# Where the split activations lie in on-chip memory: from in front of the small tiles to behind them

## The chip, the cores and the metric

The kernel runs on one core of a Trainium2 chip. The time is that of one execution on the device, in microseconds, as the median of several runs. Before the change it is 1981.72 us, the median of 3 runs from 1981.64 to 1981.88 us.

## What is computed

A decoder layer on 256 tokens of width 2048, in float32. A feed-forward layer, a mixer of two kinds of heads, and a second feed-forward layer stand one after the other, each behind a norm and added to the residual stream; a last norm follows.

```python
y = swiglu(rmsnorm(x, g1), w_gate1, w_up1, w_down1);  x = x + 0.5 * y      # 2048 -> 5632 -> 2048
y = hybrid_mixer(rmsnorm(x, g2), w_in, ..., w_out);   x = x + y            # 2048 -> 8192 columns, 2048 -> 2048
y = swiglu(rmsnorm(x, g3), w_gate2, w_up2, w_down2);  x = x + 0.5 * y
out = rmsnorm(x, final_norm)

def swiglu(h, w_gate, w_up, w_down):
    return (jax.nn.silu(h @ w_gate) * (h @ w_up)) @ w_down
```

The mixer is a retention with 4 heads and a gated linear recurrence with 8 heads on one joint projection of 8192 columns. Nearly all the work is in the products with the weights.

## The kernel before

Activations are kept transposed, a k-tile being 128 features on the partitions by 256 tokens. To multiply in nearly full float32 precision, each operand is split into a high and a low part of type fp32r, and three of the four products of parts are summed: high by high, high by low, low by high. The weights come in blocks of 128 x 1024 float32 (512 KB), one transfer each, from the SP queue into one of 6 buffers `raw` (L134). ScalarE (ACT) rounds a block to `whi` (L152), VectorE (DVE) subtracts to get `wlo` (L153); there are 4 buffers of each. Loads run 6 blocks ahead of the splits and splits up to 4 blocks ahead of the products, in the order of one flat list of (unit, block).

The split activations stand in three tiles, each with the high part and the low part of a k-tile side by side (2 x 256 columns): `xs` (16 k-tiles, 32768 bytes on each partition), written by `split_to` (L219, L220) and read by the gate and up products of both feed-forward layers and by the mixer's input projection; `hs` (44 k-tiles), read by the down products; `ms` (16 k-tiles), read by the mixer's output projection.

`run_seq` issues the products, unit by unit and block by block. A unit is one group of output columns.

- Kind T gives [columns, tokens]: the weights are stationary and the activations stream. For each k-tile and each half of the columns, L188 multiplies `whi` with both parts (512 columns in one matmul) and L189 multiplies `wlo` with the high part (256 columns). On the last k-tile the two are L191 and L192, in the other order. The last unit of the kernel uses L184 to L186 for one of its halves.
- Kind N gives [tokens, columns], for the mixer's values and output gates: a part of the activations is stationary (128 tokens) and 512 columns of `whi` or `wlo` stream, in L201, L202 and L203.

In the first stages blocks of two units (three at the start) alternate; in the down stage one unit follows the other. The norm's 1/rms is applied to the results, so products need not wait for it. `tick` counts a planned time with every product and lets the evacuation of earlier results, the mixer's small products (L615, L616, L637, L690 and others) and the splits of the next operand be issued between the products when they are due.

Tiles are laid out in the order in which their pools and they themselves are allocated: first the pool `cp` with `xT` (the residual stream), `xs` and the small tiles, then the pool `wp` with `raw`, `whi` and `wlo`, then `ev` for results, then the pool of the stage with `hs`, or `mg`, `ms` and the mixer's tiles. In the built program, in bytes on a partition:

| tile | address | remainder of 256 | with the change |
|---|---|---|---|
| xT | 16512 | 128 | the same |
| xs | 32896 | 128 | 38112, remainder 224 |
| gain, ident, ones, onesr, acc, rn, mh, rb, lb, ol, lm, le1, le0 | 65664 to 70879 | 128 for gain, 0 for ident, ones, onesr, acc | 32896 to 38111, the same remainders |
| raw (6 of 4096) | from 70880 | 224 | the same |
| whi (4 of 4096) | from 95456 | 224 | the same |
| wlo (4 of 4096) | from 111840 | 224 | the same |
| the split of e (L610, L612) | from 128256 | 0 | the same |
| hs | 136512 | 64 | the same |
| ms | 152896 | 64 | the same |

Each k-tile of `xs`, `hs` and `ms` is 2048 bytes, each stationary tile of `whi` or `wlo` 512 bytes, so every tile that one matmul reads starts at its buffer's remainder.

Of the kernel before, what the change touches and what calls it, by code (L numbers as in the profile page):

```python
# [7 lines left out]
F32 = mybir.dt.float32  # L8
F32R = mybir.dt.float32r
# [6 lines left out]
P = 128  # L16
D = 2048
S = 256
FF = 5632
KD = D // P  # L20
# [11 lines left out]


class Unit:
    """One group of output columns: kind T gives [cols, tokens], kind N gives [tokens, cols]."""

    def __init__(self, kind, w, col, ktiles, src, evac):
        self.kind, self.w, self.col, self.kt = kind, w, col, ktiles
# [6 lines left out]
class Layer:  # L45
# [14 lines left out]
            pass  # L60

    def tick(self, ns):
        """Products run without a pause; the work that hangs on them is emitted between them when it is due."""
        self.clock += ns
        due = [t for t in self.tasks if t[0] <= self.clock]
        for t in due:
            self.tasks.remove(t)
            self._step(t)
# [5 lines left out]
    def build(self):  # L74
        nc, tc, ctx, a = self.nc, self.tc, self.ctx, self.a
        cp = ctx.enter_context(tc.tile_pool(name="cp", bufs=1))
        self.wp = ctx.enter_context(tc.tile_pool(name="wp", bufs=1))
        self.ev = ctx.enter_context(tc.tile_pool(name="ev", bufs=4))
        self.pu = ctx.enter_context(tc.tile_pool(name="pu", bufs=3, space=bass.MemoryType.PSUM))
        self.pm = ctx.enter_context(tc.tile_pool(name="pm", bufs=2, space=bass.MemoryType.PSUM))  # L80
        self.xT = cp.tile([P, KD, S], F32, name="xT")
        self.xs = cp.tile([P, KD, 2, S], F32R, name="xs")
        self.gain = cp.tile([P, 6, KD], F32, name="gain")
        self.ident = cp.tile([P, P], F32, name="ident")
        self.ones = cp.tile([P, P], F32, name="ones")
        self.onesr = cp.tile([P, P], F32R, name="onesr")
        self.acc = cp.tile([P, 2, S], F32, name="acc")
        self.rn = cp.tile([P, 2], F32, name="rn")
        self.mh = cp.tile([P, 4], F32, name="mh")
        self.rb = cp.tile([P, S], F32, name="rb")  # L90

        ffn = lambda i: self.ffn_units(i)
        f1 = ffn(1)
        mx = self.mix_units()
        f2 = ffn(2)
        self.sched = f1 + mx + f2
        flat = []
        for kind, item in self.sched:
            if kind == "seq":
                flat += item  # L100
        self.flat = flat
        self.n_dma = 0
        self.n_split = 0
        self.blocks = {}
        self.pos = 0

        nc.gpsimd.memset(self.ones, 1.0)
        nc.vector.memset(self.acc[:, 0, :], 0.0)
        nc.gpsimd.memset(self.mh, -0.5)
        nc.vector.tensor_copy(self.onesr, self.ones)  # L110
        nc.sync.dma_start(self.gain, a["gains"])
        self.ahead_dma(1)
        for c in range(1, 8):
            self.x_load(c)
            self.ahead_dma((0, 2, 3, 4, 5, RAW_BUFS, RAW_BUFS, RAW_BUFS)[c])
        nc.sync.dma_start(self.ident, a["ident"])
        self.warm_up()
        self.lower_bound(cp)
        self.spawn(self.first_x())
        for kind, item in self.sched:  # L120
            if kind == "seq":
                self.run_seq(item)
            elif kind == "call":
                item()
        self.drain()

# [1 line left out]
    def ahead_dma(self, upto):  # L128
        nc = self.nc
        while self.n_dma < min(upto, len(self.flat)):  # L130
# [29 lines left out]
    def run_seq(self, steps):  # L160
        nc = self.nc
        for u, b in steps:
# [8 lines left out]
                u.cols = cols  # L171
            k0, end = b * u.per, b == u.nblk - 1
            if u.kind == "T":
                # The last block goes column by column, so that the first column's result is out early.
                turns = [(i, f) for f in range(2) for i in range(4)] if end else [(i, f) for i in range(4) for f in range(2)]
                for n, (i, f) in enumerate(turns):
                    if n == 4 and end and u.early:
# [29 lines left out]

    @staticmethod
    def order(units, turns=2):
        """Blocks in turn, those of the first units by turns: what they wait for last is needed late."""  # L210
        s = [(u, b) for b in range(units[0].nblk) for u in units[:turns]]
        for u in units[turns:]:
            s += [(u, b) for b in range(u.nblk)]
        return s

# [1 line left out]
    def split_to(self, hi, lo, src, g):  # L217
        nc = self.nc
        nc.scalar.activation(hi, src, AF.Copy, scale=g)  # L219
# [14 lines left out]
            self.split_to(self.xs[:, k, 0, :], self.xs[:, k, 1, :], self.xT[:, k, :], self.gain[:, g, k : k + 1])  # L234

    def add_out(self, ps, c, scale):
        """x += scale * (both halves of a T result)."""
        x = self.xT[:, 2 * c : 2 * c + 2, :]
        for h in (slice(0, S), slice(S, None)):
            self.nc.vector.scalar_tensor_tensor(x, ps[:, :, h], scale, x, op0=ALU.mult, op1=ALU.add)  # L240

    def warm_up(self):
        """Products of nothing while the first loads are under way, so that TensorE runs at its full clock after them."""
        pw = self.pm.tile([P, 512], F32, name="pw", tag="pm")
        for _ in range(WARM):
            self.nc.tensor.matmul(pw[:, 0:S], self.ones, self.acc[:, 0, :], start=True, stop=True)

    def preload(self, func):
        """The table of the next phase's function, while ScalarE has time."""
        t = self.ev.tile([P, 1], F32, name="pre", tag="pre", bufs=1)  # L250
        self.nc.scalar.activation(t, self.mh[:, 0:1], func)

    def lower_bound(self, cp):
        """Softmax of the logits over one layer and the reserved slot: lb, and ol = 1 - lb."""
        nc = self.nc
        lg = self.gain[:, 4, 0:8]
        self.lb, self.ol = cp.tile([P, 8], F32, name="lb"), cp.tile([P, 8], F32, name="ol")
        m, e1, e0 = (cp.tile([P, 8], F32, name=n) for n in ("lm", "le1", "le0"))
        nc.vector.tensor_scalar(m, lg, 0.0, None, op0=ALU.max)
        nc.vector.tensor_tensor(e1, lg, m, op=ALU.subtract)  # L260
        nc.scalar.activation(e1, e1, AF.Exp)
        nc.scalar.activation(e0, m, AF.Exp, scale=-1.0)
        nc.vector.tensor_tensor(m, e1, e0, op=ALU.add)
        nc.vector.reciprocal(m, m)
        nc.vector.tensor_tensor(self.lb, e1, m, op=ALU.mult)
        nc.vector.tensor_tensor(self.ol, e0, m, op=ALU.mult)

    def x_done(self, c, g):
        """The chunk of the residual stream is final: its part of the next norm and of the next operand."""
        yield LAT  # L270
        if c < 7:
            yield LAT
        self.squares(c)
        self.x_split(c, g)
        if c == 7:
            yield from self.norm_chain()
# [2 lines left out]
        self.nc.sync.dma_start(self.xT[:, 2 * c : 2 * c + 2, :], self.a["xt"][:, 2 * c : 2 * c + 2, :])  # L279

    def first_x(self):
        """The first operand, a pair of k-tiles ahead of the products that need it."""
        self.ahead_split(1)
        self.x_split(1, 0)
        self.ahead_split(2)
# [8 lines left out]
        yield from self.norm_chain(3500.0)  # L294

    def norm_chain(self, wait=6500.0):
        """1/rms of every token: per partition (rn) and along the free axis on all partitions (rb)."""
        nc = self.nc
        self.r_ready = False
        yield LAT  # L300
# [27 lines left out]
        return r.unsqueeze(1).broadcast_to([P, 2, S])  # L328

    def take(self, ps, r=True):  # L330
        """Sum of the two halves of a T result, times 1/rms."""
        nc = self.nc
        c = self.ev.tile([P, 2, S], F32, name="c", tag="ev")
        nc.scalar.copy(c, ps[:, :, S:])  # L334
# [4 lines left out]
            yield TAKE[1]  # L339
        return c  # L340

# [1 line left out]
    def ffn_units(self, i):  # L343
        st = {}

# [81 lines left out]
            self.nc.tensor.matmul(self.ss[:, t, 0:2], part[:, t * P : (t + 1) * P], self.ones[:, 0:2], **flags)  # L427

    def finish(self, ps):
        """The last chunk, the last norm and the output."""  # L430
        nc = self.nc
        last = self.finish_column(ps, 1)
        self.add_ss(self.acc[:, 0, :], start=True, stop=False)
# [13 lines left out]
            nc.vector.tensor_tensor(o[:, 0:n, :], self.xT[:, k : k + n, :], prb.unsqueeze(1).broadcast_to([P, n, S]), op=ALU.mult)  # L447
            nc.sync.dma_start(self.out[:, k : k + n, :], o[:, 0:n, :])

# [1 line left out]
    def mix_units(self):  # L451
        st = {}
        self.mx = st
# [139 lines left out]
        return [("call", open_), ("seq", steps + self.order(w)), ("call", close)]  # L593

    def hgrn(self, g, q):
        """Causal gated linear recurrence of two heads: the decay between a key and a query is a product of
        forget gates cut at the middle of the smallest aligned block that holds both. The earlier halves of the two
        blocks of 128 tokens lie in different rows, so one product serves both."""
        nc, st = self.nc, self.mx
        p = st["p"]  # L600
        f, K = st[f"f{g}"], st[f"key{g}"]
# [16 lines left out]
        nc.vector.copy_predicated(A.rearrange("p h (c t) -> p (h c) t", c=2), own, pd.rearrange("p h (c t) -> p (h c) t", c=2))  # L618

        def half(t, s, c, late):  # L620
            """The earlier or later halves of block c's sub-blocks of 2s tokens; block 1 is stored last token first."""
            return t.rearrange("p h (c m b r) -> p h c m b r", c=2, b=2, r=s)[:, :, c, :, c ^ late, :]

        tot = f.rearrange("p h (c m) -> p h c m", c=2)
# [92 lines left out]
    Layer(ctx, tc, a, out).build()  # L717


# The second block of 128 tokens is kept last token first.  # L720
ORDER = np.concatenate([np.arange(P), np.arange(S - 1, P - 1, -1)])


def _constants():
    """Tables that depend on shapes alone."""
    half = 128
    inv = np.power(np.float32(10000.0), -np.arange(0, 256, 2, dtype=np.float32) / np.float32(256))
    ang = (np.arange(S, dtype=np.float32)[:, None] * inv.astype(np.float32)[None, :]).astype(np.float32)
# [21 lines left out]


def _tiles(w, kt, cols):
    """[K, N] -> [N/cols, K/(128 kt), 128, kt*cols]: one contiguous block for each load."""
    k, n = w.shape
    return np.ascontiguousarray(w.reshape(k // (P * kt), kt, P, n // cols, cols).transpose(3, 0, 2, 1, 4)).reshape(
        n // cols, k // (P * kt), P, kt * cols)
# [40 lines left out]
```

## Time and profile before

| | |
|---|---|
| median of 3 runs | 1981.72 us |
| span of the profiled execution | 1980.3 us |
| PE busy (matmuls) | 1965.1 us, 99%, 11110 |
| PEld busy (weight loads) | 1713.0 us, 87% |
| DVE busy | 1199.7 us, 61% |
| ACT busy | 914.9 us, 46% |
| read from memory (HBM) | 365.02 MB, 185 GB/s over the span |

The page gives no other time for the profiled execution than its span; the median lies 1.4 us above it. The end of a matmul is modelled and matmuls are pipelined, so the busy time of PE and the duration of one matmul overlap with the next: the pace is to be read from the starts of matmuls or from how many of them lie in a stretch, not from the sum of their durations.

### The profile page before, as it was taken

How to read it: one execution, taken by the hardware profiler on the slowest of the kernel's cores; microseconds unless marked ns; L12 is line 12 of the kernel's file. 1: busy time of each engine (PE TensorE's matmuls, PEld its weight loads, DVE VectorE, ACT ScalarE, POOL GpSimd, SP SyncE). 2: the span in 40 equal slices, each digit the busy share in tenths (PEclk: the TensorE clock that was granted, in tenths of full speed). 3: DMA queues.
4: the chain of work that ended last, by engine and by line, in shares of the span. 5: the costliest groups of instructions: out<-in, count | busy, mean ns of one | idle time of the engine just before them, and what ended most of it. 6: DMA issues, size and time to landing. Idle time of an engine off the chain costs nothing.

```text
span 1980.3 us, 27797 instructions
## 1 busy us (share of the span) xinstructions
PE 1965.1 (99%) x11110; PEld 1713.0 (87%) x11110; DVE 1199.7 (61%) x1472; ACT 914.9 (46%) x1102; POOL 20.0 (1%) x28
## 2 busy tenths in 40 slices
PE   9999999999999999999999999999999999999997
PEld 7888888888888888888888888888888888888887
DVE  7666565666545546777766666565666656545544
ACT  6444444444444444545344454444444444434432
POOL 0000000000000000000000000000000000000000
PEclk9999999999999999999999999999999999999999
DMA  7555555555555556444555555555555555555552
GB/s 272 192 186 191 191 192 188 187 191 191 191 185 188 192 184 231 160 170 160 171 170 177 183 182 184 188 190 192 185 190 191 192 191 186 188 190 191 184 190 96
DMA packets 102625, 368.93 MB, mean 186 GB/s; under 512 B 11552, under 2 KB 11936, under 8 KB 102496
## 3 DMA queue, kind: packets, MB, share of 16 engines
q1 hardware_dynamic: 101952, 365.06, 54.2%
q0 software_dynamic: 544, 2.10, 0.3%
q8 instruction: 87, 1.43, 0.3%
q14 instruction: 42, 0.34, 0.0%
HBM read 365.02 MB, written 2.10 MB: 185 GB/s over the span
## 4 chain that ended last, share of the span: by engine, by line
PE 98%; DMA 0%; DVE 0%; ACT 0%; SPq 0%; issue 0%; POOLq 0%; DVEq 0%
PE ups L188 54%; PE ups L189 28%; PE ups L203 3%; PE ups L201 3%; PE ups L202 3%; PE ups L192 3%; PE ups L191 2%; PE pa L637 1%; DMA xT<-in_xt 0%; PE ups L186 0%; PE ups L184 0%; PE ups L185 0%; DVE o L447 0%; PE pt L563 0%; PE psc L690 0%; PE po L667 0%
## 5 line engine op out<-in xcount | busy, mean ns | idle before, releaser
L153 DVE TENSOR_TENSOR wlo<-raw,whi 128x1024 fp32r<-128x1024 f32 (+1 forms) x689 | 841.0, 1222 | 678.1 <-ACT whi L152 677.7
L188 PE MATMUL ups<-xs,whi 128*128 128x512 f32 x3120 | 1098.2, 393 | 1.7 <-DVE xs L220 1.3
L152 ACT CAST whi<-raw 128x1024 fp32r<-128x1024 f32 (+1 forms) x689 | 722.0, 1049 | 680.5 <-PE ups L188 433.8
L189 PE MATMUL ups<-xs,wlo 128*128 128x256 f32 x3120 | 874.1, 280 | 1.5 <-DVE wlo L153 1.5
L188 PEld LDWEIGHTS ups<-xs,whi 128*128 128x128 f32 x3120 | 585.9, 188 | 124.0 <-DVE xs L220 2.2
L189 PEld LDWEIGHTS ups<-xs,wlo 128*128 128x128 f32 x3120 | 586.6, 188 | 11.1 <-DVE wlo L153 2.1
L188 PE MATMUL ups<-hs,whi 128*128 128x512 f32 x1333 | 469.6, 393 | 0.0
L189 PE MATMUL ups<-hs,wlo 128*128 128x256 f32 x1333 | 372.5, 279 | 0.0
L188 PEld LDWEIGHTS ups<-hs,whi 128*128 128x128 f32 x1333 | 250.0, 188 | 56.2
L189 PEld LDWEIGHTS ups<-hs,wlo 128*128 128x128 f32 x1333 | 250.0, 188 | 1.5
L334 ACT COPY c<-ups 128x512 f32<-128x512 f32 x104 | 60.8, 585 | 179.4 <-PE ups L192 177.5
L201 PE MATMUL ups<-whi,xs 128*128 128x512 f32 x256 | 103.2, 403 | 0.0
L203 PE MATMUL ups<-wlo,xs 128*128 128x512 f32 x256 | 101.5, 396 | 0.0
L202 PE MATMUL ups<-whi,xs 128*128 128x512 f32 x256 | 100.7, 393 | 0.0
L188 PE MATMUL ups<-ms,whi 128*128 128x512 f32 x240 | 85.0, 394 | 0.0
L192 PE MATMUL ups<-xs,whi 128*128 128x512 f32 x208 | 81.9, 394 | 0.0
L336 DVE TENSOR_TENSOR c<-ups,c 128x512 f32<-128x512 f32 x104 | 71.2, 684 | 0.0
L372 ACT CAST hs<-c 128x512 fp32r<-128x512 f32 x44 | 27.3, 621 | 93.1 <-DVE c L369 93.1
L338 DVE TENSOR_TENSOR c<-c,rb 128x512 f32<-128x512 f32 x96 | 66.5, 693 | 3.3
L189 PE MATMUL ups<-ms,wlo 128*128 128x256 f32 x240 | 67.1, 280 | 0.0
L203 PEld LDWEIGHTS ups<-wlo,xs 128*128 128x128 f32 x256 | 48.1, 188 | 11.7
L191 PE MATMUL ups<-xs,wlo 128*128 128x256 f32 x208 | 58.2, 280 | 0.0
(148 smaller groups left out, 908.9 us busy)
## 6 DMA issues: line engine op xcount, KB each, us to landing
raw<-in_u SPq DMA_DIRECT2D x176, 512.0 KB, 3.3
raw<-in_d SPq DMA_DIRECT2D x176, 512.0 KB, 3.3
raw<-in_g SPq DMA_DIRECT2D x175, 512.0 KB, 3.3
raw<-in_wit SPq DMA_DIRECT2D x64, 512.0 KB, 3.3
raw<-in_win SPq DMA_DIRECT2D x64, 512.0 KB, 3.4
raw<-in_wo SPq DMA_DIRECT2D x32, 512.0 KB, 3.4
xT<-in_xt SPq DMA_DIRECT2D x8, 256.0 KB, 7.6
out_y<-o SPq DMA_DIRECT2D x7, 256.0 KB, 2.4
```

Source lines behind the costliest of these rows:

```text
L152: nc.scalar.copy(hi[:, c], raw[:, c])
L153: nc.vector.tensor_tensor(lo[:, c], raw[:, c], hi[:, c].bitcast(F32), op=ALU.subtract)
L188: nc.tensor.matmul(full, wh, src[:, k, :, :], start=first, stop=False)
L189: nc.tensor.matmul(half, wl, src[:, k, 0, :], start=False, stop=False)
L191: nc.tensor.matmul(half, wl, src[:, k, 0, :], start=False, stop=False)
L192: nc.tensor.matmul(full, wh, src[:, k, :, :], start=False, stop=True)
L201: nc.tensor.matmul(o, xh, wh, start=k == 0, stop=False)
L202: nc.tensor.matmul(o, xl, wh, start=False, stop=False)
L203: nc.tensor.matmul(o, xh, wl, start=False, stop=k == u.kt - 1)
L334: nc.scalar.copy(c, ps[:, :, S:])
L336: nc.vector.tensor_tensor(c, ps[:, :, 0:S], c, op=ALU.add)
L338: nc.vector.tensor_tensor(c, c, self.rb2(), op=ALU.mult)
```

## The change

The allocation of `xs` moves from behind `xT` to behind the small tiles, and the five small tiles of the lower bound, which were allocated in `lower_bound`, are now allocated with the other small tiles, ahead of `xs`. So `xs` ends where the first `raw` begins, and since it is 128 times 256 bytes long, it starts at the remainder of 256 of the weights' buffers. No instruction changes, and none changes its place in its engine's order.

```diff
         self.xT = cp.tile([P, KD, S], F32, name="xT")
-        self.xs = cp.tile([P, KD, 2, S], F32R, name="xs")
         self.gain = cp.tile([P, 6, KD], F32, name="gain")
...
         self.rb = cp.tile([P, S], F32, name="rb")
+        self.lbt = [cp.tile([P, 8], F32, name=n) for n in ("lb", "ol", "lm", "le1", "le0")]
+
+        self.xs = cp.tile([P, KD, 2, S], F32R, name="xs")
...
-        self.lower_bound(cp)
+        self.lower_bound()
...
-    def lower_bound(self, cp):
+    def lower_bound(self):
...
-        self.lb, self.ol = cp.tile([P, 8], F32, name="lb"), cp.tile([P, 8], F32, name="ol")
-        m, e1, e0 = (cp.tile([P, 8], F32, name=n) for n in ("lm", "le1", "le0"))
+        self.lb, self.ol, m, e1, e0 = self.lbt
```

## Rows read from the trace of the kernel before

**Rows 1.** The page: busy time of each engine, and clock in 40 slices.
```profile
PE 1965.1 (99%) x11110; PEld 1713.0 (87%) x11110; DVE 1199.7 (61%) x1472; ACT 914.9 (46%) x1102; POOL 20.0 (1%) x28
PE   9999999999999999999999999999999999999997
PEclk9999999999999999999999999999999999999999
```
**Rows 2.** Groups by line, shapes apart: busy us, mean ns | idle before, releaser.
```profile
L188 PE MATMUL ups<-xs,whi 128*128 128x512 f32 x3120 | 1098.2, 393 | 1.7 <-DVE xs L220 1.3 <-ACT whi L152 0.4
L189 PE MATMUL ups<-xs,wlo 128*128 128x256 f32 x3120 | 874.1, 280 | 1.5 <-DVE wlo L153 1.5
...
L188 PE MATMUL ups<-hs,whi 128*128 128x512 f32 x1333 | 469.6, 393 | 0.0
L189 PE MATMUL ups<-hs,wlo 128*128 128x256 f32 x1333 | 372.5, 279 | 0.0
...
L201 PE MATMUL ups<-whi,xs 128*128 128x512 f32 x256 | 103.2, 403 | 0.0
L203 PE MATMUL ups<-wlo,xs 128*128 128x512 f32 x256 | 101.5, 396 | 0.0
L202 PE MATMUL ups<-whi,xs 128*128 128x512 f32 x256 | 100.7, 393 | 0.0
...
L192 PE MATMUL ups<-xs,whi 128*128 128x512 f32 x208 | 81.9, 394 | 0.0
...
L192 PE MATMUL ups<-hs,whi 128*128 128x512 f32 x31 | 12.4, 398 | 0.0
```
**Rows 3.** Windows, PE alone: stretch, length, busy (matmuls), clock, DMA; streams xs, hs, xs, ms.
```profile
110.00:450.00 340.00, 340.00 (x1959) 1.00 0.56 190
510.00:725.00 215.00, 215.00 (x1229) 1.00 0.55 189
1330.00:1670.00 340.00, 340.00 (x1959) 1.00 0.56 190
1150.00:1230.00 80.00, 80.00 (x458) 1.00 0.56 191
```
**Rows 4.** Timeline of PE in kind N: start us, us, instruction; 18 matmuls apart.
```profile
1109.69 0.40 PE L203 MATMUL ups<-wlo,xs 128*128 128x512 f32 x1
...
1113.89 0.40 PE L203 MATMUL ups<-wlo,xs 128*128 128x512 f32 x1
```
**Rows 5.** Timeline of PE: one head's scores, plain float32.
```profile
1028.86 1.03 PE L690 MATMUL psc<-rot 128*128 128x256 f32 x4
1029.73 0.61 PE L692 MATMUL psc<-rot 128*128 128x128 f32 x4
```
**Rows 6.** Timeline: a product and the weight load of the next one.
```profile
299.87 0.28 PE L189 MATMUL ups<-xs,wlo 128*128 128x256 f32 x1
299.88 0.19 PEld L191 LDWEIGHTS ups<-xs,wlo 128*128 128x128 f32 x1
```
**Rows 7.** Durations of L615, L616, L188 and L201: ns min/median/max, first and last start.
```profile
L615 PE MATMUL pd<-e,onesr x4: 395/395/398, 786.8 to 930.9; 128*128 128x512 f32 x4
...
L616 PE MATMUL pd<-e,onesr x4: 394/396/397, 787.1 to 931.1; 128*128 128x512 f32 x4
...
L188 PE MATMUL ups<-xs,whi x3120: 390/392/587, 6.2 to 1719.7; 128*128 128x512 f32 x195
...
L201 PE MATMUL ups<-whi,xs x256: 389/398/583, 770.0 to 1138.8; 128*128 128x512 f32 x128
```

## Prediction

> **What bounds the kernel now.** I read the busy times and the 40 slices first: PE is busy for 1965.1 of the 1980.3 us of the span, in every slice but the last, at a granted clock of 9 tenths or more throughout [rows 1]. DVE and ACT stand at 61% and 46%. The groups by line come next: for all its 3120 products with `xs` as the moving operand, L188 shows 1.7 us of idle time before it, and L189 1.5 us; the products with `hs` show none [rows 2]. So nearly nothing that DVE, ACT or a transfer does can shorten the span, and nothing that they do is on the path but the first and the last few microseconds. What counts is how fast products follow each other, and the third view, the number of matmuls in long windows, gives that. All of TensorE's work below comes in pairs of one matmul of 512 and one of 256 columns, 768 columns together, or in triples of three times 512.
>
> - `xs` as the moving operand: 1959 matmuls in 340 us, which is 173.55 ns each or **347.1 ns a pair**, and the window from 1330 us gives the same count [rows 3].
> - `hs`: 1229 in 215 us, **349.9 ns a pair**; `ms`: 458 in 80 us, 349.3 ns [rows 3].
> - Kind N, where `xs` is stationary and a weight tile streams: from the matmul of L203 at 1109.69 us to the one 18 matmuls later at 1113.89 us are 4.20 us, 233.3 ns each, or 350.0 ns for 768 columns [rows 4].
>
> The windows' clock is 1.00, the 2.4 GHz level, at which 768 columns take 320.0 ns. So there are 27 to 30 ns in each pair that are neither columns nor clock nor a wait, and they differ with the operand although the instructions have the same shapes. The reader should also see that plain float32 products lack them: the four records of L690, two passes of 256 columns each by their length, take from 1028.86 to 1029.73 us, some 217 ns for 512 columns [rows 5]. And the weights of the next product are loaded while this one streams: the load of L191 and the product of L189 before it start 0.01 us apart [rows 6]. Two reads of the same memory run side by side, and that is where an address can matter.
>
> **The change part by part.** No instruction is added, removed or moved on any engine or queue; the sequence of each engine, waits included, is the same. What moves is memory. The small tiles sink by 32768 bytes, a multiple of 256, and keep their remainders; `xT`, `raw`, `whi`, `wlo`, `hs` and `ms` stay. `xs` alone changes its remainder: it lay at 128 and the weights at 224, so the moving operand started 96 bytes below the stationary one; now both are at 224, a distance of 0. `hs` and `ms` lie at 64, which is 96 bytes above the weights (64 + 256 - 224). In kind N the roles are swapped, so the moving tile lies 96 above the stationary one. Sorted by that distance the trace reads: **-96: 347.1 ns; +96: 349.9, 349.3 and 350.0 ns**. Three streams of different stages agree at +96, one at -96 differs.
>
> The splits of `xs` on ACT and DVE are 48 and 48 instructions off the path (the wait on them is the 1.7 us above) and I cost their new place at nothing: if each became 10% slower, 48 x 0.05 us of engines that are busy for 61% at most would still be hidden, and of the first k-tiles, which PE does wait for, it would be under 0.1 us. The five tiles of the lower bound are only allocated earlier: nothing.
>
> What is left is the pace of the products that read `xs`. There are 3120 pairs of L188 and L189 and 208 of L191 and L192, 3328 together [rows 2], or 1155 us at 347.1 ns, and 768 products of kind N, which are 384 times 768 columns.
>
> No steady row shows distance 0. From below, the 27 ns over 320.0 could go altogether: 3328 x 27.1 = 90 us. One row stands against this: L615 and L616 multiply `onesr` with the split `e`, both at remainder 0, and their durations of 395 and 396 ns are no shorter than the 392 of L188 with `xs` [rows 7]; durations follow the pace (L201 at 398 [rows 7] and L192 with `hs` at 398 [rows 2] have the longer steps). So the overhead stays at distance 0 in substance, at least for single products between others. From above, those 3 ns more would be paid by each 512-column product: 3328 x 3 = 10 us. The nearest measure for how much a place can change a stream is the step between -96 and +96, 2.8 ns a pair. I take one such step, **downwards**, 344.3 ns. Two things speak for it, neither strongly: in the same position of the program, the last product of a block, the one that starts at -96 (L192 with `xs`) takes 394 ns, the one at +96 (L192 with `hs`) 398 [rows 2], so that the place matters there too, and the one row at 0 lies near the good end. And in kind N the distance of +96, the bad one, is removed altogether, which can hardly cost.
>
> Sum: 3328 x -2.8 = -9.3 us; kind N from 350.0 to 344.3, 384 x -5.7 = -2.2 us; all else 0. That is -11.5 us. The profiled execution has a span of 1980.3 us, the median of the runs is 1981.72, so 1.4 us lie around the span and don't change: **1970.2 us**.
>
> The SBUF page of the Trainium skill ("SBUF — State Buffer", the section on the two sides) says that PE has ports of its own and never waits on another engine, and the TensorE page ("TensorE: Matmul & The Clock Gate", Part 2) that these are two independent read ports, one for the moving operand, one for LDWEIGHTS. By this rule the two reads couldn't disturb each other, the remainder would be worth nothing and the time would stay at 1981.7 us. The trace's 2.8 ns between `xs` and `hs` at equal shapes and clock speak against it. The same TensorE page (Part 1) gives N/2.4 + 2.5 ns from product to product, an estimate of 325 ns for a pair; the windows show 347.1 and 349.9.
>
> **The rivals.**
>
> 1. *It is where the moving tile starts, not its distance to the weights* (slower). The same rows sort that way just as well: moving tiles at remainder 128 (`xs`) run at 347.1, those at 64 (`hs`, `ms`) and at 224 (kind N) at 349.3 to 350.0. Then `xs` at 224 takes the pace of these: 3328 x 2.8 = +9.3 us, kind N unchanged, **1991.0 us**. It decides as soon as pairs with `xs` show more than 347.1 ns. For it: L615's 395 at distance 0. Against it: 64 and 224 have little in common but that they aren't multiples of 128. To it I add that distance 0 lies between -96 and +96 and the pace too, 348.5 ns (+4.7 us, less 0.6 in kind N: 1985.8 us), and that equal remainders make the two reads meet more often than at either, a step beyond `hs` (352.7 ns, +18.6 us, 2000 us).
> 2. *The place is worth nothing* (no change). The pace would belong to something else in which the stages differ, such as the alternation of two units in the gate and up stage against one unit at a time in the down stage. Here belongs the rule of the independent ports. Against it: `ms` has the alternation of two units like `xs`, and the pace of `hs`. **1981.7 us**, or 1980 if only kind N gains.
> 3. *The overhead goes in good part* (faster by more). If the weight load and the stream run in step from equal remainders, and half of the 27 ns is what their meeting costs, 3328 x 13.5 = 45 us, 1937 us. L615 speaks against it.
>
> That the change doesn't do what it says I leave out: the addresses of the built program show it.
>
> **How the numbers follow.** About 0.2% (4 us) is what a measurement of this kernel can tell from no change. Forecast 0.42, rival 3 0.05: faster 0.47. Rival 2: 0.20. Rival 1: 0.33, of which 0.20 for the start of the moving tile, 0.08 for the pace in between, 0.05 for a step beyond. The forecast's own range is 1962 to 1977.7: two such steps for the pairs and -2.2 for kind N at one end (1981.7 - 18.6 - 2.2 = 1960.9, rounded to the near side), the 0.2% at the other. The whole range goes from there to rival 1's price with a microsecond more, 1992, and leaves out rival 3 and the step beyond, 0.10 together.
>
> **What would show it.** In the windows 110 to 450 us and 1330 to 1670 us the count of matmuls should rise from 1959 to about 1975 (680000/344.3); at rival 1 it falls to 1943. In the `hs` stretch the pace must stay at 349.9 ns, since nothing there is moved; if it changes, something other than the remainder of `xs` is at work. Kind N should go from 233.3 to about 229.5 ns a product, and L201 lose its median of 398 ns. ACT and DVE durations, transfers and clock should be as before; if PE shows idle time, or a clock under 1.00, my reading of the bound is wrong. The forecast is wrong if `xs` pairs come out at or above 347 ns.

## The result: 13.9 us slower, and two opposite moves inside it

| | before | with the change |
|---|---|---|
| median of 5 runs | 1981.72 us (1981.59 to 1981.98) | 1995.58 us (1995.22 to 1996.06) |
| ratio | 1 | 1.0070, 95% interval 1.0057 to 1.0082 |
| span of the profiled execution | 1980.3 us | 1993.7 us |

The page of the changed kernel shows the same bound as [rows 1], busy in every slice but the last, at full clock:

```profile
PE 1979.2 (99%) x11110; PEld 1715.7 (86%) x11110; DVE 1198.9 (60%) x1472; ACT 914.5 (46%) x1102; POOL 20.0 (1%) x28
PEclk9999999999999999999999999999999999999999
```

The groups of instructions by line (line, engine, operation, tiles, shape, count | busy us, mean ns | idle before), two lines further down in this source, so that L190 is the L188 of before, L194 is L192, and L203 to L205 are L201 to L203:

```profile
L190 PE MATMUL ups<-xs,whi 128*128 128x512 f32 x3120 | 1114.5, 399 | 1.1 <-DVE xs L222 0.6 <-ACT whi L154 0.5
L191 PE MATMUL ups<-xs,wlo 128*128 128x256 f32 x3120 | 876.2, 281 | 1.4 <-DVE wlo L155 1.4
L190 PE MATMUL ups<-hs,whi 128*128 128x512 f32 x1333 | 469.6, 393 | 0.0
L203 PE MATMUL ups<-whi,xs 128*128 128x512 f32 x256 | 101.8, 398 | 0.0
L205 PE MATMUL ups<-wlo,xs 128*128 128x512 f32 x256 | 99.9, 390 | 0.0
L204 PE MATMUL ups<-whi,xs 128*128 128x512 f32 x256 | 99.7, 390 | 0.0
...
L194 PE MATMUL ups<-xs,whi 128*128 128x512 f32 x208 | 83.1, 400 | 0.0
```

Against [rows 2], the 512-column product with `xs` is 6 ns longer (L190 and, as the last of a block, L194), the one with `hs` is unchanged at 393, and kind N is 3 to 6 ns shorter. No idle time has come in. The windows, PE alone, over the stretches of [rows 3] that fed on `xs`, `hs` and `xs`:

```profile
110.00:450.00 340.00, 340.00 (x1927) 1.00 0.58 186
510.00:725.00 215.00, 215.00 (x1230) 1.00 0.58 187
1330.00:1670.00 340.00, 340.00 (x1927) 1.00 0.57 186
```

1927 matmuls instead of 1959 in 340 us: **352.9 ns a pair instead of 347.1**, while `hs` keeps its 349.6 to 349.9. And the timeline of PE in kind N, 21 matmuls apart, where [rows 4] has 233.3 ns each:

```profile
1111.65 0.39 PE L205 MATMUL ups<-wlo,xs 128*128 128x512 f32 x1
...
1116.41 0.39 PE L205 MATMUL ups<-wlo,xs 128*128 128x512 f32 x1
```

4.76 us / 21 = **226.7 ns**. The account: 3328 pairs x 5.8 ns = +19.3 us, 768 products of kind N x -6.6 ns = -5.1 us, +14.2 in all, an estimate from the steady stretches, where the median moved by 13.9 and the span by 13.4. The starts of the stages in the two traces bear it out: the first gate and up stage is 7.6 us longer, the mixer's input projection, which has pairs and kind N, 2.3 us shorter, the second gate and up stage 8.1 us longer, and the stages that read `hs` and `ms` are the same. So the whole difference lies in the pace of the products that read `xs`, and nothing else moved.

### The profile page after: what moved, and what is told of

It reads as the page before. It is cut to its first block, busy times and chain, and to the rows that moved or that the text cites. A ratio compares the mean times of both kernels' runs of the same rounds, so it can differ in the third digit from the quotient of the medians.

```text
span 1993.7 us, 27797 instructions
## 1 busy us (share of the span) xinstructions
PE 1979.2 (99%) x11110; PEld 1715.7 (86%) x11110; DVE 1198.9 (60%) x1472; ACT 914.5 (46%) x1102; POOL 20.0 (1%) x28
## 4 chain that ended last, share of the span: by engine, by line
PE 98%; DVE 0%; DMA 0%; ACT 0%; SPq 0%; issue 0%; POOLq 0%; DVEq 0%
PE ups L190 55%; PE ups L191 28%; PE ups L194 3%; PE ups L205 3%; PE ups L203 3%; PE ups L204 3%; PE ups L193 2%; PE pa L638 1%; DMA xT<-in_xt 0%; PE ups L188 0%; PE ups L186 0%; PE ups L187 0%; DVE o L448 0%; PE pt L564 0%; PE psc L691 0%; PE po L668 0%
## 5 line engine op out<-in xcount | busy, mean ns | idle before, releaser
L190 PE MATMUL ups<-xs,whi 128*128 128x512 f32 x3120 | 1114.5, 399 | 1.1 <-DVE xs L222 0.6
L190 PEld LDWEIGHTS ups<-xs,whi 128*128 128x128 f32 x3120 | 586.2, 188 | 135.6 <-DVE xs L222 1.6
L190 PE MATMUL ups<-hs,whi 128*128 128x512 f32 x1333 | 469.6, 393 | 0.0
L190 PEld LDWEIGHTS ups<-hs,whi 128*128 128x128 f32 x1333 | 250.0, 188 | 56.4
L203 PE MATMUL ups<-whi,xs 128*128 128x512 f32 x256 | 101.8, 398 | 0.0
L205 PE MATMUL ups<-wlo,xs 128*128 128x512 f32 x256 | 99.9, 390 | 0.0
L190 PE MATMUL ups<-ms,whi 128*128 128x512 f32 x240 | 84.9, 394 | 0.0
L194 PE MATMUL ups<-xs,whi 128*128 128x512 f32 x208 | 83.1, 400 | 0.0
L205 PEld LDWEIGHTS ups<-wlo,xs 128*128 128x128 f32 x256 | 48.0, 188 | 10.3
```

Source lines behind the costliest of these rows:

```text
L190: nc.tensor.matmul(full, wh, src[:, k, :, :], start=first, stop=False)
L194: nc.tensor.matmul(full, wh, src[:, k, :, :], start=False, stop=True)
L203: nc.tensor.matmul(o, xh, wh, start=k == 0, stop=False)
L205: nc.tensor.matmul(o, xh, wl, start=False, stop=k == u.kt - 1)
```

## The experiments

"Distance" is always the start of the moving tile less the start of the stationary one, by remainders of 256 bytes, from -128 to 124. Pace from windows is 2 x length / count; where a stage is too short for a window, the mean or median of the steps between matmul starts in the trace is given. Where a single time is given, the kernel was run once.

**Where the tile starts, or how far from the weights.** Two kernels separate what the change joined. In the first, from the kernel before, the weights come to `xs`:

```diff
-        m, e1, e0 = (cp.tile([P, 8], F32, name=n) for n in ("lm", "le1", "le0"))
+        m, e1, e0 = (self.ev.tile([P, 8], F32, name=n, tag=n, bufs=1) for n in ("lm", "le1", "le0"))
```

> The kernel before, with three 32-byte tiles allocated behind the weights' buffers, so that raw, whi and wlo start at remainder 128, where xs already is; xs, hs and ms do not move. Theory A (what counts is the distance of the moving tile's start from the start of the weight tile, in remainders of 256): xs pairs go from 347 to about 353 ns as in the changed kernel, kind N from 233 to about 227 ns a product, and hs and ms, which now lie at -64 instead of +96 without having moved, leave 350 ns; the time is about 1995 us plus or minus what hs gives. Theory B (what counts is where the moving tile itself starts): xs stays at 347 and hs and ms at 350 ns, kind N, whose moving tiles now start at 128, comes near 231.5 ns; the time is 1980 to 1982 us.

In the second, from the changed kernel, a gap brings back the old distances at new places:

```diff
         self.xs = cp.tile([P, KD, 2, S], F32R, name="xs")
+        cp.tile([P, 24], F32, name="gap")
```

> The changed kernel with 96 bytes left free between xs and the weights' buffers, so that xs stays at remainder 224 and everything behind it moves to other remainders with the old distances (xs -96, hs and ms +96). Theory A: every pace of the kernel before comes back (xs 347 ns a pair, hs and ms 350, kind N 233 a product) and the time is 1981.7 us within 1 us. Theory B: xs, still at 224, keeps 353 ns, kind N moves, and the time stays above 1990 us.

Measured: 2000.53 and 1982.45 us, beside 1981.92 of the kernel before. The windows of PE, `xs` and `hs`, in the first kernel:

```profile
110.00:450.00 340.00, 340.00 (x1926) 1.00 0.54 186
510.00:725.00 215.00, 215.00 (x1219) 1.00 0.54 187
```

and in the second:

```profile
110.00:450.00 340.00, 340.00 (x1959) 1.00 0.56 190
510.00:725.00 215.00, 215.00 (x1230) 1.00 0.55 189
```

In the first `xs` lies where it always lay and still loses the 347 ns (1926, one less than the changed kernel); `hs` has not moved either and goes from 349.9 to 352.7 ns. In the second, with `xs` at 224 as in the change, the old counts are back to within one. Theory A holds, theory B falls.

**Which load, and whose traffic.** From the changed kernel, `wlo` alone put 96 bytes higher:

```diff
+            if self.n_split == 0:
+                self.wp.tile([P, 24], F32, name="gap", tag="gap", bufs=1)
             lo = self.wp.tile([P, 1024], F32R, name="wlo", tag="wlo", bufs=SPL_BUFS)
```

> The changed kernel with 96 bytes left free between the buffers of whi and those of wlo: for xs, whi stays at distance 0 and wlo goes back to -96. While a product of 512 columns with whi streams, the next weights loaded are wlo; while one of 256 columns with wlo streams, they are whi. If a stream meets the load that runs beside it, the products of 512 columns go back from a mean of 237 to about 230 ns and those of 256 stay near 117.5 ns, some 347 to 349 ns a pair. If the weights in use count (the tile that the product itself multiplies), the products of 512 columns, whose own weights are at 0, stay at 237 ns. In kind N the products with whi stay near 227 ns, the one with wlo goes to 231 to 238 ns.

Measured: 1988.73 us, 351 ns a pair in the gate and up stages. The step from the start of a 512-column product to the next product has a mean of 233.6 ns there: more than the 229.7 of the kernel before, which has the same distance to `wlo`, and less than the 235.8 of the changed one, which has the same distance to `whi`. And `hs`, with whi at -64 and wlo at +96, gets 346.8 ns a pair, shorter than with either distance for both (353.2 and 350.0). Neither expected answer fits: the pace depends on the two distances together, not on one load for each product.

From the changed kernel, only the first 12 blocks of weights are loaded and split; the products after them use the last four again and again:

```diff
         while self.n_split < min(upto, len(self.flat)):
+            if self.n_split >= 12:
+                self.blocks[self.n_split] = self.kept[self.n_split % SPL_BUFS]
+                self.n_split += 1
+                continue
...
-            self.ahead_dma(self.n_split + RAW_BUFS)
+            self.ahead_dma(min(12, self.n_split + RAW_BUFS))
```

> The changed kernel with the loads and splits of the weights left out after the first 12 blocks, the products using the same four buffers again and again: ACT, DVE and the DMA queues no longer touch the weights' buffers, and the output is of the wrong weights. If the pace is an affair of TensorE's two reads alone, xs stays near 353 ns a pair, hs and ms at 350, kind N near 227 ns a product, and the time within some us of 1994. If writes by ACT, DVE or DMA into the same memory are what disturbs the stream, all paces fall towards 325 ns a pair and the time by up to 100 us.

Measured: 1995.38 us. Its page, and its windows of PE for `xs` and `hs` (the last two columns are DMA share and GB/s):

```profile
PE 1979.1 (99%) x11110; PEld 1715.8 (86%) x11110; DVE 407.8 (20%) x796; ACT 227.8 (11%) x426; POOL 16.3 (1%) x28
```

```profile
110.00:450.00 340.00, 340.00 (x1927) 1.00 0.00 1
510.00:725.00 215.00, 215.00 (x1230) 1.00 0.00 1
```

DVE has lost two thirds of its work, ACT three quarters, the DMA all, and both counts are those of the changed kernel. So the loss doesn't come from what other engines or transfers do to the weights' buffers. With the two kernels above, which tie it to the distance of the two tiles that TensorE reads, TensorE's own reads are what is left.

**The scan.** `xs` goes behind so many of the 32-byte tiles, `hs` behind an unused tile. For the second run, from the changed kernel (the lines that go are left out):

```diff
+        self.lbt = [cp.tile([P, 8], F32, name=n) for n in ('lb', 'ol', 'lm', 'le1')]
+        self.xs = cp.tile([P, KD, 2, S], F32R, name="xs")
...
+            p.tile([P, (192, 128)[i - 1] // 4], F32, name=f"gap{i}")
             st["hs"] = p.tile([P, KF, 2, S], F32R, name=f"hs{i}")
```

> The kernel before with xs 32 bytes higher (distance -64 to the weights), hs of the first feed-forward at distance 0 and hs of the second at distance 256, by unused tiles in front. If the distance decides and repeats every 256 bytes: xs goes to the 353 ns a pair that hs and ms showed at -64, both hs stages to about 352 to 353 ns as xs had at 0, equal to each other. If 512 bytes (the size of one weight tile) is the period, the second hs stage differs from the first. If xs and hs differ for another reason than distance (alternating units), hs at 0 does not show the pace of xs at 0.

> Scan of the distance: xs at +32, hs of the first feed-forward at +32, hs of the second at -32, kind N at -32 (its moving tile lies that far from its stationary one). By distance alone the first two show one pace. Between the known points (-64: 353, 0: 352 to 353, +96: 350 ns a pair) a smooth curve would give 351 to 353 at +32 and 353 at -32; a collision of two reads that lock in step may jump instead, anywhere from 343 to 357. Kind N from 680 ns a triple at 0 upwards.

> Scan of the distance: xs at 128, hs of the first feed-forward at 128, hs of the second at +64, kind N at 128. By distance alone the first two show one pace. A smooth curve between -96 (347 ns a pair) and +96 (350) around the far side gives 347 to 350 at 128, and 350 to 352 at +64; the shortest pair of the whole scan would then lie near -96 to 128.

> Scan of the distance: xs at -32, hs of the first feed-forward at -64, hs of the second at -96, kind N at +32. By distance alone hs at -64 repeats 353 ns a pair and hs at -96 the 347 ns of xs in the kernel before, which would also make the second down stage about 700 x 2.8 = 2 us shorter; xs at -32 repeats what hs of the second feed-forward shows at -32 in the run beside this one.

Measured: 2001.32, 1980.51, 1995.03 and 2000.65 us, beside 1982.61. Pace by distance, mean of the steps from one 512-column product to the next:

| distance | -96 | -64 | -32 | 0 | +32 | +64 | +96 | 128 |
|---|---|---|---|---|---|---|---|---|
| `xs`, ns a pair | 347.3 | 352.9 | 352.5 | 352.3 | 347.1 | 353.2 | 350.3 | 350.7 |
| `hs`, ns a pair | 346.9 | 353.2 | 353.2 | 353.2 | 346.8 | 350.7 | 350.0 | 351.2 |
| kind N, ns a triple (median) | 702 | 700 | 699 | 680 | 700 | 687 | 700 | 696 |

(Kind N at -96 and -64 and `xs` at +64 and +96 come from the fine scan below.) `xs` and `hs` agree within 1 ns but at +64, where `hs` itself shows 350.7 here and 353.1 in the fine scan. `hs` at distance 256 repeats distance 0: both 353.18. But there is no smooth curve. The windows of the second run, `xs` and `hs`, show the +32 that the interpolation had put at 351 to 353:

```profile
110.00:450.00 340.00, 340.00 (x1960) 1.00 0.56 190
510.00:725.00 215.00, 215.00 (x1242) 1.00 0.55 191
```

**The fine scan.** Tiles of `whi` and `wlo` get 256 bytes more, 5 raw buffers make the room, and each unit has its own offset:

```diff
+            u = self.flat[self.n_split][0]
-            hi = self.wp.tile([P, 1024], F32R, name="whi", tag="whi", bufs=SPL_BUFS)
+            hi = self.wp.tile([P, 1088], F32R, name="whi", tag="whi", bufs=SPL_BUFS)[:, u.oh : u.oh + 1024]
```

(and `lo` likewise with `u.ol`).

> A fine scan in one run: the kernel before with tiles of whi and wlo that are 256 bytes longer (and 5 raw buffers instead of 6 for the room), in which every unit of output columns uses its own offset, equal for whi and wlo. The gate and up units go through all 64 distances of xs in steps of 4 bytes, the down units through 16 distances of hs in steps of 16 bytes, the kind N units through 0, 16, 48, 64, 80, -96, -64 and -16. If the pace follows 16-byte lines of memory, the curve is flat within 16 bytes and changes between lines; if it follows the exact start, it changes every 4 bytes. At distances that were run before the known paces come back (-96: 347, 0: 353, +32: 347 ns a pair; kind N at 0: 680 ns a triple). A place below 345 ns a pair would be one that neither kernel uses; the time of this run is a mean over all of them, about 1995 us.

> The same form with whi and wlo at offsets of their own: the 64 pairs of distances in steps of 32 bytes for xs, 16 pairs in steps of 64 bytes for hs. If each stream meets the load that runs beside it and nothing else, the 512-column step depends on the distance to wlo alone and the 256-column step on that to whi alone. If the two reads lock over the whole pair of products, only combinations have a pace; from the run with 96 bytes between whi and wlo, whi 0 with wlo -96 gives 351 ns a pair and whi -64 with wlo +96 gives 347.

Measured: 1990.9 and 1986.89 us. Of the expected answers the second is nearest each time, and too simple. The pace changes with steps of 4 bytes: with `xs` 349.5 ns at +48, 347.8 at +52, 350.0 at +56, 347.3 at +60, 353.2 at +64. With `hs`, 84 pairs to a place, most means gather near 346.8, 350.0 and 353.2, some 3.2 ns apart. In the second scan there is no separate effect of either load: with `xs`, moving wlo from +96 to 0 takes 6 ns off a pair where whi is at -96 (353.1 to 346.9) and adds 6 ns where it is at 0 (347.1 to 352.9). The lowest combination that both operands show is whi -96 with wlo -32: **343.6 ns with `hs`, 344.1 with `xs`**.

A few places gave two answers: +16 is 346.7 with `hs` and 352.0 with `xs`; whi -32 with wlo -32 is 346.8 with `hs` in this scan and 353.2 in the last; whi -64 with wlo +96, at 346.8 with `hs` in the kernel with the gap in front of `wlo`, is 352.7 with `xs`. And whi +64 with wlo 0 is 347.3 ns where it alternates with another unit at the start of the second gate and up stage, but goes below all else at the end of the first, where the timeline shows it at 340 ns a pair, 24 pairs in 8.16 us:

```profile
493.01 0.39 PE L205 MATMUL ups<-xs,whi 128*128 128x512 f32 x1
...
501.17 0.39 PE L205 MATMUL ups<-xs,whi 128*128 128x512 f32 x1
```

Each unit of the scans runs behind a unit of other distances, so a value here belongs to that sequence and not surely to the distance alone.

**Does kind N's gain stand alone?** Every block of kind N is written 160 bytes higher, in the longer tiles and with the 5 raw buffers of the scans, all else as before:

```diff
+        for u, _ in flat:
+            u.oh, u.ol = (0, 0) if u.kind == "T" else (40, 40)
```

> The kernel before with 256 bytes more in every tile of whi and wlo (and 5 raw buffers), used only by the blocks of kind N, which are written 160 bytes higher, so that in kind N the moving tile starts at the remainder of xs: distance 0 there, -96 for xs as before. If the gain of kind N in the changed kernel belongs to the distance alone, kind N shows 680 ns a triple, all pairs of 768 columns keep their 347 and 350 ns, and the time falls by 256 x 17 ns = 4 us to about 1977.5 us. If the room taken from the raw buffers costs something, the time is higher and PE shows idle time.

Measured: 1978.18 us (10 runs), ratio to before **0.9979, interval 0.9970 to 0.9988**. The half of the change that was a gain can be had without the half that was a loss; kind N shows 680 ns a triple, and `xs` and `hs` their old paces.

**The lowest combination, in all stages.** `u.oh, u.ol = (0, 48)` for kind T, kind N as in the last run, and 64 bytes ahead of `hs` and `ms`:

> The same, and for the products with moving activations whi stays at -96 and wlo goes to -32, the lowest combination of the scan (343.6 ns a pair with hs, 344.1 with xs); hs and ms are put 64 bytes higher, to the remainder of xs. Expected by the scan: xs 347.3 to 344.0 ns on 3328 pairs (-11 us), hs and ms 350.0 to 343.6 on some 1600 pairs (-10 us), kind N -4 us; together about 1956 us, below both kernels. If locked steps do not carry over from the scan's short stretches, the pairs are at 347 to 353 ns and the time is 1975 us or more.

Measured: 1989.93 us, where 1956 was expected, as the median of six, five of them at 1989.45 to 1990.39 and one at 1977.13; ratio 1.0040 (1.0026 to 1.0053). The windows of PE in the execution of 1977.13, first `xs` and `hs`, then the second `xs` and `hs`:

```profile
110.00:450.00 340.00, 340.00 (x1937) 1.00 0.54 188
510.00:725.00 215.00, 215.00 (x1225) 1.00 0.54 188
...
1330.00:1670.00 340.00, 340.00 (x1974) 1.00 0.55 191
1750.00:1920.00 170.00, 170.00 (x991) 1.00 0.55 192
```

The same layout, the same instructions, and 351.1 ns a pair in the first feed-forward layer against 344.5 (`xs`) and 343.1 (`hs`) in the second. The steps between matmul starts tell where it turned: the output projection still ends at 351.7 ns a pair; then come the first two units of the second gate and up stage, whose blocks alternate, with the norm's small products between them; from the third unit on, at 1256 us, it is 344.5. So a distance alone doesn't set a pace: the same distances allow two that last. The five slower executions were not profiled; that their second layer stayed at the longer pace is possible, but not shown.

**What decides between the two.** Two more kernels: one with -96 everywhere and kind N at 0, one with the lowest combination and a unit of other distances early in each stage:

```diff
+        units = lambda *w: [u for n, u in enumerate(u for u, b in flat if b == 0) if u.w in w]
+        for u in (units("g1", "u1")[3], units("g2", "u2")[2], units("wo")[2]):
+            u.oh, u.ol = 56, 40
```

> The kernel with kind N at distance 0 and xs at -96, and hs and ms put 64 bytes higher, so that they lie at -96 too. Every run so far gave 347 ns a pair at -96, with xs and with hs. If the pace follows the distances and -96 has one pace, hs and ms go from 350 to 346.8 ns, 1450 pairs with hs and 256 with ms, -5.5 us against the kernel with kind N alone: about 1973 us, the same in every run. If -96 has a second pace as well, the runs spread over 10 us as those of the last kernel did.

> The kernel with whi at -96 and wlo at -32, in which one unit early in each feed-forward stage and in the output projection is put at -64 and 0, the distances of the unit after which the scan had shown 344 ns. If the same distances have two lasting paces (352 and 344 ns) and what went before decides which, the first feed-forward stage goes to 344 ns after that unit and stays there, hs follows, and the time is 1956 to 1962 us in every run. If the pace is drawn anew in each execution and not by the unit before, some runs stay near 1990 us. If the first feed-forward stage stays at 352 ns, the entry is not what decides.

Measured: **1972.47 us** (1972.25 to 1972.63, four runs; ratio 0.9950, 0.9935 to 0.9965) and **1961.93 us** (1961.11 to 1962.55, four runs; ratio 0.9897, 0.9881 to 0.9914). The windows of PE in the second kernel, as above:

```profile
110.00:450.00 340.00, 340.00 (x1974) 1.00 0.57 192
510.00:725.00 215.00, 215.00 (x1252) 1.00 0.56 192
...
1330.00:1670.00 340.00, 340.00 (x1974) 1.00 0.56 190
1750.00:1920.00 170.00, 170.00 (x997) 1.00 0.56 191
```

Now both feed-forward layers run at 343 to 344.5 ns in the profiled execution, and the times of the other three agree with it. In the first layer one unit out of 44 put the rest on the shorter pace; for the second it is not shown that the unit was needed, since the kernel without it ran at 344.5 ns there in its execution of 1977.13 us. The unit itself, whi -64 with wlo 0, ran at 340 ns a pair in the first layer, again 24 pairs in 8.16 us:

```profile
45.19 0.39 PE L194 MATMUL ups<-xs,whi 128*128 128x512 f32 x1
...
53.35 0.39 PE L194 MATMUL ups<-xs,whi 128*128 128x512 f32 x1
```

In the second layer the same unit took 349.9 ns. Whether 340 ns can be made to last, no run here tries. Both kernels are faster than before and than the change. The work is the same in each: the same products in the same order.

## Why the prediction was wrong

- *What bounds the kernel* was right: the count of matmuls in windows, not busy times or waits, carries the whole result.
- *Only the distance changes, and it matters by itself* was right: moving the weights to `xs` makes the loss (1926), giving back the distance takes it away (1959).
- **The step that failed** is the sign and size of one term: "I take one such step, **downwards**, 344.3 ns". The pairs with `xs` went up by 5.8 ns instead of down by 2.8, +19.3 us where -9.3 stood. The two reasons given for "downwards" could not bear it. L192 with `xs` showed only which of -96 and +96 is the better place; at distance 0 it went from 394 to 400 ns itself. L615 at distance 0 is a single product between others: its 395 ns are less than the 399 of the products with `xs` that follow each other at that distance. And the size, the step between -96 and +96, is no measure for a third distance: +32 and -32, as far from 0, are 5 to 6 ns apart. No row told which way 0 would go.
- *Kind N* had the right sign and was mis-sized: -5.1 us instead of -2.2. Part of that is a slip: 768 products of 512 columns are 512 times 768 columns, not 384, so its own pace of 344.3 ns gives -2.9 us, and the forecast by its own terms would have been 1969.5 us. The rest is the pace, 226.7 ns a product instead of 229.5.
- *Rival 1* came out on the right side, by the wrong mechanism. Its start of the moving tile, 1991.0 us, is refuted by the first two experiments. What it only added, that equal remainders cost a step beyond `hs` (352.7 ns), is the pace measured (352.9), but with kind N unchanged it would have given 2000 us; and equal remainders as such are not the cause, since kind N is shortest there.
- *Rival 2*, no change, is refuted. What it took from the rule of the two independent read ports, that where the tiles lie is worth nothing, fails: the pace follows the distance between the two tiles that PE reads. What the SBUF page of the Trainium skill says beside it ("SBUF — State Buffer", the section on the two sides), that PE waits for no other engine's accesses, agrees with the run without loads and splits: 1927 and 1230 matmuls with and without that traffic.
- A premise of rival 2, that `ms` alternates two units like `xs`, was wrong, and so is the description ahead: only the first two or three units of a gate and up stage or of a projection alternate; `order` (L209) takes all others one after the other, as in the down stage. The stages differ less than was said, and the scans, where `xs` and `hs` agree at most distances, fit that.

## What to carry to other kernels

Where PE is busy throughout, compare the pace of products of equal shape between stages first: 1% between two operands, at equal clock and without waits, was here a question of where they lie, and one look at a shifted layout answers it better than an argument from neighbouring distances. Test the layout for each kind of product apart, since the remainder that served kind N harmed kind T. And time a chosen layout in several executions: a lasting pattern can depend on the products before it, and a unit of other distances in front may be what keeps the good one.

## What was not expected of the hardware

Starts that differ by 4 bytes gave paces up to 7 ns apart in 350 (354.3 at -20, 346.8 at -24 in the fine scan). The paces of `hs` mostly lie some 3.2 ns apart (343.6, 346.8, 350.0, 353.2). The same distances can run at two paces, 351 to 352 and 344 ns, over hundreds of microseconds in one execution, and what was multiplied before can decide which. Why the fp32r products that follow each other lose 20 to 34 ns beyond the 320 of their columns and the plain float32 ones of [rows 5] hardly any, and what in the memory makes the pattern, no run here shows; that stays open, as does why one of six executions without the unit in front was shorter than the other five.
